# The transposes of an attention layer's keys and queries share the PSUM bank of the values' products

## The chip, the cores and the metric

The kernel runs on one core of a Trainium2 chip. The metric is the device time of one execution in microseconds; the kernel before took 1372.63 us in the median of three runs (1371.01 to 1373.25). The core has five engines that work side by side: TensorE (PE) multiplies matrices and writes only to PSUM, VectorE (DVE) and ScalarE (ACT) read PSUM and compute elementwise, GpSimd (POOL) does a little set-up, and SyncE (SP) issues the transfers. PSUM holds eight banks of 128 partitions by 512 float32 values in this kernel's tiles, and one tile takes one bank.

## What is computed

The reference is a decoder trunk of two layers over 512 tokens of width 1024. The first layer mixes two kinds of state-space heads, the second is a latent attention with 16 heads; each is followed by a SwiGLU network. The change is in the attention layer only:

```python
q = (rms_norm(cq, q_lora_norm) @ w_uq).reshape(bsz, seqlen, H, MLA_NOPE + MLA_ROPE)
kv = (rms_norm(ckv, kv_lora_norm) @ w_ukv).reshape(bsz, seqlen, H, MLA_NOPE + MLA_V)
...
s = jnp.einsum('bqhd,bkhd->bhqk', qn, k_nope) + jnp.einsum('bqhr,bkr->bhqk', qr, k_rope)
s = s.astype(jnp.float32) * scale
...
p = jax.nn.softmax(jnp.where(mask, s, -jnp.inf), axis=-1).astype(v.dtype)
return jnp.einsum('bhqk,bkhv->bqhv', p, v)
```

A head has 64 elements with a norm and 32 with a rotary position (the rotary key is shared by all heads), and its values have 64. The mask is causal.

## The kernel before

All tokens are one tile of 512 columns. A dense product in near float32 precision is done as three matmuls of the fp32r type: weight and activation are each split into a high and a low part, and high by high, high by low and low by high are added up in one accumulator (`mm3`, L149 to L152). The weights come by transfer into `wraw`, ACT rounds them to `whi` (L144) and DVE forms `wlo` (L145). The accumulators are a ring of three PSUM banks, `acc()` (L63), that the whole kernel uses.

The attention layer opens five more banks (L710): two for scores (`sco`), two for transposed probabilities (`ptr`) and one for the products of the values (`po`, reached by `aux("po")`). Three and five make eight: PSUM is full.

Heads are taken in pairs, eight pairs in all. `project(g)` (L826) makes queries, keys and values of two pairs with dense products, and then normalises them and applies the rotary part on DVE. `prepare` (L875) turns one pair's keys (one tile for both heads) and queries (one tile for each head) with PE transposes into three PSUM tiles. ACT and DVE copy the keys to `kT` (L886, L888), ACT copies the queries to `qT` (L894). There are four `kT` and four `qT` buffers, enough for two pairs. `attend` (L898) does four blocks of queries: scores (L911), mask and maximum on DVE (L914), exponential on ACT (L916), division on DVE (L922), transposes of the probabilities (L925) and a copy of them on ACT (L929). At the end come the products with the values in `po` (L934), and `split` empties that bank (ACT L126, then DVE L127). `o_round(r)` (L944) is the output projection over four pairs.

The code asks for the work in this order (L957 to L968): `project(0)`, `project(1)`, `prepare` of pair 0, and then for each pair p: `prepare` of pair p+1, `attend` of pair p, a `project` after pairs 0 and 2 (`PROJ`), and `o_round(0)` after pair 4. `o_round(1)` follows the loop.

Nothing in the code fixes the order within an engine. A planner takes, each time an engine is free in its own model of the times, the instruction that the code asked for first among those that are ready; the loading of weights is put 90 places ahead (`AHEAD`, L132). On the chip each engine then works through its list in that order, and waits on semaphores. A ring of PSUM banks is handed out in the order in which the code asks for its tiles: a tile waits until the one that had its bank has been read for the last time.

Of the kernel before, what the change touches and what calls it, by code (L numbers as in the profile page):

```python
# [46 lines left out]
def kernel(ctx: ExitStack, tc: tile.TileContext, A, yT, stop=99):  # L47
# [11 lines left out]
    def nm(s):  # L59
        cnt[0] += 1  # L60
        return f"{s}_{cnt[0]}"

    def acc():  # L63
        return pacc.tile([P, T], F32, tag="acc", name=nm("acc"))
# [11 lines left out]
    def aux(tag="st"):  # L76
        while isinstance(phase["tags"][tag], str):
            tag = phase["tags"][tag]
        return phase["p"].tile([P, T], F32, tag=tag, name=nm(tag), bufs=phase["tags"][tag])
# [17 lines left out]
    ps = acc()  # L97
# [3 lines left out]
    def col(name, i=0, lo=0, hi=P):  # L101
        j = PV[name] + i
        return pv[lo:hi, j:j + 1]
# [182 lines left out]
    with tc.tile_pool(name="gkp", bufs=1) as gkp:  # L286
        rtok = tok_scalar(R)

        ps = aux("a1")
# [15 lines left out]
        ps = aux()  # L305
# [26 lines left out]
        ps = aux()  # L332
# [6 lines left out]
        ps = aux()  # L339
# [168 lines left out]
        with tc.tile_pool(name="gla", bufs=2) as gp:  # L508
# [16 lines left out]
            for h in range(4):  # L525
                ps = aux()
# [186 lines left out]
    with tc.tile_pool(name="mla", bufs=2) as mp, tc.tile_pool(name="mla1", bufs=1) as m1:  # L713
# [30 lines left out]
        ps = acc()  # L744
# [10 lines left out]
        for who, n0, n in (("q", 0, 3), ("kv", 3, 2)):  # L755
            lora[who], ssq = [], None
            for c in range(n):
                w = weight(A["w_dqkv"][n0 + c], KD, P)
                ps = acc()
# [12 lines left out]
            ps = aux()  # L772
# [22 lines left out]
        ps = aux()  # L795
# [14 lines left out]
        ps = aux()  # L810
# [63 lines left out]

        def prepare(g, hp, qs, ks, v):  # L875

            ps = acc()
            for i in range(4):
                E.transpose(ps[:, i * P:(i + 1) * P],
                            ks[:, i, 2 * hp:2 * hp + 2, :].rearrange("p h d -> p (h d)"), ident)  # L880
            kts, qts = [], []
            for j in range(2):
                t = kT[(4 * g + 2 * hp + j) % NK]
                kts.append(t)
                if j == 0:
                    S.activation(t[0:64, :], ps[0:64, :], AF.Copy, scale=col("k_gain", 0, 0, 64))  # L886
                else:
                    V.tensor_scalar(t[0:64, :], ps[64:P, :], col("k_gain", 0, 64, P), None, ALU.mult)  # L888
            for j in range(2):
                ps = acc()  # L890
                for i in range(4):
                    E.transpose(ps[0:96, i * P:(i + 1) * P], qs[:, i, 2 * hp + j, :], ident)
                qT = mp.tile([96, T], F32, tag="qT", name=nm("qT"), bufs=4)
                S.activation(qT, ps[0:96, :], AF.Copy, scale=col("q_gain", 0, 0, 96))  # L894
                qts.append(qT)
            return kts, qts
# [59 lines left out]

        pr = {0: project(0), 1: project(1)}  # L957
        ready = prepare(0, 0, *pr[0])
        for p in range(8):
            g, hp = divmod(p, 2)  # L960
            cur = ready
            if p < 7:
                ready = prepare((p + 1) // 2, (p + 1) % 2, *pr[(p + 1) // 2])
            attend(g, hp, pr[g][2], *cur)
            if p in PROJ:
                pr[2 + PROJ.index(p)] = project(2 + PROJ.index(p))
            if p == 4:
                o_round(0)  # L968
# [89 lines left out]
```

## Time and profile before

| | |
|---|---|
| median of three runs | 1372.63 us |
| profiled execution, its own time | 1371.09 us |
| span from its first to its last instruction | 1368.9 us |
| PE busy | 1344.9 us, 98% |
| DVE, ACT busy | 815.5 us, 562.8 us |
| transposes of keys and queries | about 834 to 958 us of the span |
| products of the values (eight pairs) | 860.5 to 988 us |
| granted PE clock | 0.999 |

Times in the profile are counted from the span's first instruction. A row in order of time gives start, duration, engine, line, operation, the tiles written and read, shape and count; in brackets stands the idle time of the engine ahead of it and what ended that. Rows of one line that follow each other are merged. PEld is the loading of the stationary operand, which runs beside the matmuls. A matmul of float32 operands leaves two records.

### The profile page before, as it was taken

What the parts mean: (1) busy time and instruction counts of PE and PEld (TensorE: products, weight loads), DVE (VectorE), ACT (ScalarE), POOL (GpSimd) and SP (SyncE); (2) the same over time, 40 slices, a digit from 0 to 9 for tenths busy, and PEclk for the clock granted to TensorE, in tenths of its full rate; (3) what the DMA queues carried; (4) which work ended last, traced back from release to release, by engine and by line L of the source; (5) the groups of instructions that cost most, each with busy time, mean ns of one, the idle gap of its engine ahead of it and who ended that gap; (6) DMA issues with size and microseconds to landing.
All of it is one profiled execution on the core that took longest, in us unless ns stands there. A gap on an engine that the chain in (4) does not pass through costs nothing.

```text
span 1368.9 us, 16667 instructions
## 1 busy us (share of the span) xinstructions
PE 1344.9 (98%) x6506; PEld 1088.7 (80%) x6506; DVE 815.5 (60%) x1369; ACT 562.8 (41%) x941; POOL 7.8 (1%) x35
## 2 busy tenths in 40 slices
PE   8999999999999999999999999999999999999998
PEld 5788889788888888888888887666588888888887
DVE  7987976788867444444333469776594444443221
ACT  5584633544344322332232348775653322322121
POOL 0000000000000000000000000000000000000000
PEclk9999999999999999999999999999999999999999
DMA  5342232222233333223333321111033223323331
GB/s 177 109 141 91 77 95 78 78 77 62 79 93 105 93 94 106 92 92 99 90 100 100 101 68 56 39 47 62 1 98 103 93 93 102 98 93 108 111 103 63
DMA packets 36781, 122.22 MB, mean 89 GB/s; under 512 B 4768, under 2 KB 5792, under 8 KB 36704
## 3 DMA queue, kind: packets, MB, share of 16 engines
q1 hardware_dynamic: 35888, 120.72, 28.1%
q8 instruction: 51, 0.84, 0.2%
q10 hardware_dynamic: 816, 0.46, 0.1%
q14 instruction: 26, 0.21, 0.0%
HBM read 119.03 MB, written 2.13 MB: 89 GB/s over the span
## 4 chain that ended last, share of the span: by engine, by line
PE 90%; DVE 5%; ACT 3%; issue 1%; DMA 1%; SPq 0%; ACTq 0%
PE acc L150 27%; PE acc L151 27%; PE acc L152 27%; PE sco L911 2%; PE ptr L925 1%; PE po L934 1%; DVE wlo L145 1%; PE a L447 1%; PE a L625 0%; PE a L433 0%; PE a L614 0%; PE a L451 0%; ACT whi L144 0%; PE a L627 0%; DVE gm L534 0%
## 5 line engine op out<-in xcount | busy, mean ns | idle before, releaser
L150 PE MATMUL acc<-xh,whi 128*128 128x512 f32 x1144 | 449.1, 393 | 5.2 <-DVE dp L322 2.5
L144 ACT CAST whi<-wraw 128x1024 fp32r<-128x1024 f32 (+2 forms) x221 | 225.8, 1022 | 554.0 <-PE acc L151 436.9
L151 PE MATMUL acc<-xl,whi 128*128 128x512 f32 x1144 | 448.7, 392 | 0.0
L152 PE MATMUL acc<-xh,wlo 128*128 128x512 f32 x1144 | 448.7, 392 | 0.0
L145 DVE TENSOR_TENSOR wlo<-wraw,whi 128x1024 fp32r<-128x1024 f32 (+2 forms) x221 | 261.9, 1185 | 163.2 <-ACT whi L144 163.1
L150 PEld LDWEIGHTS acc<-xh,whi 128*128 128x128 f32 x1144 | 214.9, 188 | 51.2 <-ACT cvt L366 2.8
L152 PEld LDWEIGHTS acc<-xh,wlo 128*128 128x128 f32 x1144 | 215.1, 188 | 44.8 <-DVE wlo L145 0.6
L151 PEld LDWEIGHTS acc<-xl,whi 128*128 128x128 f32 x1144 | 215.1, 188 | 44.5 <-issue 1.4
L152 PE MATMUL acc<-fhh,wlo 128*128 128x512 f32 x288 | 112.0, 389 | 0.0
L150 PE MATMUL acc<-fhh,whi 128*128 128x512 f32 x288 | 112.0, 389 | 0.0
L151 PE MATMUL acc<-fhl,whi 128*128 128x512 f32 x288 | 112.0, 389 | 0.0
L683 DVE TENSOR_TENSOR fu<-acc,R 128x512 f32<-128x512 f32 x44 | 30.4, 691 | 136.2 <-PE acc L152 136.2
L680 DVE TENSOR_TENSOR fg<-acc,R 128x512 f32<-128x512 f32 x44 | 30.4, 691 | 89.0 <-PE acc L152 88.9
L152 PEld LDWEIGHTS acc<-fhh,wlo 128*128 128x128 f32 x288 | 54.1, 188 | 11.3
L151 PEld LDWEIGHTS acc<-fhl,whi 128*128 128x128 f32 x288 | 54.1, 188 | 11.3
L150 PEld LDWEIGHTS acc<-fhh,whi 128*128 128x128 f32 x288 | 54.1, 188 | 11.1
L151 PE MATMUL acc<-mxl,whi 128*128 128x512 f32 x128 | 49.9, 391 | 0.0
L150 PE MATMUL acc<-mxh,whi 128*128 128x512 f32 x128 | 49.8, 391 | 0.0
L152 PE MATMUL acc<-mxh,wlo 128*128 128x512 f32 x128 | 49.7, 390 | 0.0
L911 PE MATMUL sco<-kT,qT 96*128 96x128 f32 (+3 forms) x128 | 42.8, 445 | 1.5 <-DVE mx L914 1.3
L914 DVE CUSTOM_DVE_ANT_0 sc<-sco,am 128x128 f32<-128x128 f32 (+3 forms) x64 | 30.7, 487 | 13.6 <-PE sco L911 11.5
L916 ACT ACTIVATE sc<-sc,mx 128x128 f32<-128x128 f32 (+3 forms) x64 | 35.7, 561 | 7.3 <-DVE mx L914 6.8
(329 smaller groups left out, 1584.8 us busy)
## 6 DMA issues: line engine op xcount, KB each, us to landing
wraw<-in_w_gate_dram SPq DMA_DIRECT2D x44, 512.0 KB, 3.5
wraw<-in_w_up_dram SPq DMA_DIRECT2D x44, 512.0 KB, 3.5
wraw<-in_w_down_dram SPq DMA_DIRECT2D x32, 512.0 KB, 3.6
wraw<-in_w_out_dram SPq DMA_DIRECT2D x16, 512.0 KB, 3.6
wraw<-in_w_xbc_dram SPq DMA_DIRECT2D x12, 512.0 KB, 3.6
wraw<-in_w_down_dram SPq DMA_DIRECT2D x16, 384.0 KB, 3.1
wraw<-in_w_z_dram SPq DMA_DIRECT2D x8, 512.0 KB, 3.5
wraw<-in_w_v_dram SPq DMA_DIRECT2D x8, 512.0 KB, 3.5
```

The costliest lines, as they stand in the source:

```text
L144: S.copy(hi[:, :kc * m], r)
L145: V.tensor_tensor(lo[:, :kc * m], r, hi.bitcast(F32)[:, :kc * m], ALU.subtract)
L150: E.matmul(out, ah, bh, start=first, stop=False)
L151: E.matmul(out, ah, bl, start=False, stop=False)
L152: E.matmul(out, al, bh, start=False, stop=last)
L447: E.matmul(pd[64 * h:64 * h + 64, c * P:(c + 1) * P], xdt[:, c, h, :], mt[:, h, c, :], start=True, stop=True)
L680: V.tensor_tensor(g, pg, R, ALU.mult)
L683: V.tensor_tensor(u, pu, R, ALU.mult)
L911: E.matmul(ps[:, :n], qts[j][:, b * P:(b + 1) * P], kts[j][:, :n], start=True, stop=True)
L914: V.tensor_tensor_reduce(sc[:, :n], ps[:, :n], am[:, T - n:], -scale, 3e38, ALU.add, ALU.min, mx[:, j:j + 1])
L916: S.activation(sc[:, :n], sc[:, :n], AF.Exp, bias=mx[:, j:j + 1], scale=-1.0, accum_out=sm[:, j:j + 1])
L925: E.transpose(ps[:, kb * P:(kb + 1) * P], sc[:, kb * P:(kb + 1) * P], ident)
```

## The change

The three PSUM tiles of `prepare` (one of keys, two of queries) are taken from the bank `po` instead of from the three accumulators. `po` has one bank. Everything else is as it was.

```diff
         def prepare(g, hp, qs, ks, v):
 
-            ps = acc()
+            ps = aux("po")
             for i in range(4):
                 E.transpose(ps[:, i * P:(i + 1) * P],
                             ks[:, i, 2 * hp:2 * hp + 2, :].rearrange("p h d -> p (h d)"), ident)
...
             for j in range(2):
-                ps = acc()
+                ps = aux("po")
                 for i in range(4):
                     E.transpose(ps[0:96, i * P:(i + 1) * P], qs[:, i, 2 * hp + j, :], ident)
                 qT = mp.tile([96, T], F32, tag="qT", name=nm("qT"), bufs=4)
```

## The prediction

> **What bounds the kernel now.** I read the page first (shares, the chain of work that ended last), then the busy time by stretches of the attention stage, then what TensorE (PE) waited for there, then single rows in order of time.
>
> ```profile
> span 1368.9 us, 16667 instructions
> ...
> PE 1344.9 (98%) x6506; PEld 1088.7 (80%) x6506; DVE 815.5 (60%) x1369; ACT 562.8 (41%) x941; POOL 7.8 (1%) x35
> ...
> PE 90%; DVE 5%; ACT 3%; issue 1%; DMA 1%; SPq 0%; ACTq 0%
> ```
>
> PE is busy 98% of the span and is 90% of the chain. The change adds and removes no instruction, so it can move the time only through PE's idle time, 1368.9 - 1344.9 = 24.0 us in all, and only where keys and queries are transposed. Busy time by stretch (length, then PE, PEld, DVE, ACT, POOL, granted clock):
>
> ```profile
> 834.00:842.00 8.00, 5.71 (x38) 4.35 (x36) 7.81 (x19) 6.73 (x12) 0.00 (x0) 1.00 0.36 115
> 842.00:864.00 22.00, 21.55 (x116) 16.35 (x117) 18.35 (x51) 19.54 (x45) 0.00 (x0) 1.00 0.19 58
> 864.00:878.00 14.00, 11.36 (x55) 7.39 (x53) 13.10 (x46) 8.33 (x24) 0.00 (x0) 1.00 0.10 39
> 878.00:900.00 22.00, 21.90 (x123) 15.07 (x122) 14.79 (x42) 18.34 (x45) 0.00 (x0) 1.00 0.15 49
> 900.00:914.00 14.00, 10.97 (x54) 6.68 (x53) 10.77 (x38) 11.37 (x30) 0.00 (x0) 1.00 0.12 38
> 914.00:948.00 34.00, 34.00 (x173) 24.69 (x173) 22.25 (x54) 14.83 (x36) 0.00 (x0) 1.00 0.13 44
> 948.00:962.00 14.00, 12.88 (x73) 9.07 (x72) 10.62 (x36) 11.49 (x32) 0.00 (x0) 1.00 0.16 47
> 962.00:989.00 27.00, 26.23 (x142) 15.44 (x140) 14.56 (x54) 17.52 (x51) 0.00 (x0) 1.00 0.01 1
> sum 155.00, PE 144.60 PEld 99.05 DVE 112.25 ACT 108.14 POOL 0.00; mean PE 18.07 PEld 12.38 DVE 14.03 ACT 13.52 POOL 0.00
> ```
>
> PE idles 155.00 - 144.60 = 10.4 us here: 2.3 at the start, 2.6 in 864 to 878, 3.0 in 900 to 914, 1.1 in 948 to 962, next to nothing elsewhere. What PE waited for in 834 to 992 (total, times, longest):
>
> ```profile
> PE acc L150 <- ACT qT L894: 3.0, 2, 1.6
> PE acc L879 <- ACT qT L894: 1.4, 3, 1.0
> PE acc L150 <- ACT qs L838: 0.7, 1, 0.7
> PE acc L892 <- DVE kT L888: 0.6, 1, 0.6
> PE acc L892 <- ACT v L852: 0.6, 1, 0.6
> PE acc L150 <- DVE kT L888: 0.5, 1, 0.5
> ```
>
> These six are waits for an accumulator bank to be emptied, 3.0 + 1.4 + 0.7 + 0.6 + 0.6 + 0.5 = 6.8 us, two thirds of the idle time. Why a bank is late is seen at the second pair of 860 to 878. Here prepare(n) is the preparation of pair n and po(n) its product of values; below, a hop is the hand-over of a bank from one tile to the next:
>
> ```profile
> 860.50 2.37 PE L934 MATMUL po<-pt,v 128*64 128x512 f32 x16
> ...
> 864.88 0.66 PE L879 MATMUL acc<-ident,ks 128*128 128x128 f32 x4 [0.21 <-ACT qT L894]
> ...
> 873.17 0.45 PE L150 MATMUL acc<-whi,lh 128*128 128x384 f32 x1 [1.35 <-ACT qT L894]
> ...
> 875.69 0.44 PE L150 MATMUL acc<-whi,lh 128*128 128x384 f32 x1 [0.67 <-ACT qs L838]
> ...
> 882.52 2.37 PE L934 MATMUL po<-pt,v 128*64 128x512 f32 x16
> ...
> 893.55 2.38 PE L934 MATMUL po<-pt,v 128*64 128x512 f32 x16
> ```
> ```profile
> 863.09 0.60 ACT L126 CAST xh<-po 128x512 fp32r<-128x512 f32 x1
> ...
> 871.87 0.68 ACT L886 ACTIVATE kT<-acc,pv 64x512 f32<-64x512 f32 x1 [0.17 <-PE sco L911]
> 872.45 0.67 ACT L894 ACTIVATE qT<-acc,pv 96x512 f32<-96x512 f32 x1
> ...
> 877.21 0.68 ACT L894 ACTIVATE qT<-acc,pv 96x512 f32<-96x512 f32 x1 [0.98 <-PE sco L911]
> ```
>
> prepare(3) fills three accumulators from 864.88 on, but its kT and qT buffers still belong to pair 1, whose scores come first (the releaser is the score matmul, L911). So the banks are emptied only from 871.87 to 877.89, and project(3), whose dense products stand behind them, can't start before 873.17. Three of three accumulators are parked for 7 to 13 us.
>
> **The change, part by part.** Removed: 8 x 3 = 24 claims on the accumulators. Added: 24 claims on the one bank of po, which had 8, so 32 claims in one line. Instructions, shapes, DMAs and their queues stay. The bank is handed out in the order in which the code asks: prepare(n+1) sits between po(n-1) and po(n). Nothing is parked any more: when po(n-1) is done, the scores of pair n-1, which held kT and qT, are done too.
>
> *Start* (834 to 842). Six tiles go out here, with these waits:
>
> ```profile
> 835.09 0.60 PE L879 MATMUL acc<-ident,ks 128*128 128x128 f32 x4
> 836.24 1.05 PE L892 MATMUL acc<-ident,qs 128*96 128x128 f32 x8 [0.55 <-ACT v L852]
> 838.27 0.66 PE L879 MATMUL acc<-ident,ks 128*128 128x128 f32 x4 [0.98 <-ACT qT L894]
> 840.15 0.64 PE L892 MATMUL acc<-ident,qs 128*96 128x128 f32 x4 [0.56 <-DVE kT L888]
> ```
> ```profile
> 836.68 0.95 DVE L145 TENSOR_TENSOR wlo<-wraw,whi 128x768 fp32r<-128x768 f32 x1
> ...
> 839.34 0.75 DVE L888 TENSOR_SCALAR kT<-acc,pv 64x512 f32<-64x512 f32 x1
> ...
> 859.51 0.56 DVE L145 TENSOR_TENSOR wlo<-wraw,whi 128x384 fp32r<-128x384 f32 x1 [0.81 <-ACT whi L144]
> ...
> 864.57 0.68 DVE L127 TENSOR_TENSOR xl<-po,xh 128x512 fp32r<-128x512 f32 x1
> ...
> 949.94 1.23 DVE L145 TENSOR_TENSOR wlo<-wraw,whi 128x1024 fp32r<-128x1024 f32 x1 [0.16 <-ACT whi L144]
> ```
>
> Before: 0.55 + 0.98 + 0.56 = 2.1 us idle. After: the first queries wait for the keys' second copy on DVE, which is behind other work there until 839.34 and ends at 840.1. Meanwhile project(2) may have the accumulators, but its first split weight is ready only at 836.68 + 0.95 = 837.6, while the keys' transposes end at 835.7: some 1.7 to 1.9 us idle. Gain 0.3; bounds 2.1 (all goes) and -1.0 (the delayed first scores hold up pair 0).
>
> *864 to 878.* The waits 0.21 + 1.35 + 0.67 = 2.2 us. project(3) can fill them: its queries' weights are split by 859.51 + 0.56 = 860.1, and the next stretch (21.90 of 22.00) shows that what is pulled forward shortens a full one. Gain 2.2; bounds 0 and 2.2.
>
> *900 to 914.* The one wait of 1.60:
>
> ```profile
> 913.82 0.50 PE L150 MATMUL acc<-xh,whi 128*128 128x512 f32 x1 [1.60 <-ACT qT L894]
> ...
> 951.12 0.66 PE L879 MATMUL acc<-ident,ks 128*128 128x128 f32 x4 [0.20 <-ACT qT L894]
> ...
> 959.42 0.47 PE L150 MATMUL acc<-xh,whi 128*128 128x512 f32 x1 [0.47 <-DVE kT L888]
> ```
>
> o_round(0) then has three accumulators at once and 3 banks x 3 ready inputs x 3 matmuls = 27 dense matmuls to put into its gaps. But pair 3 is itself bound by its chain through DVE and ACT here, and dense work used early is missing at 914 to 921. Gain 1.1; bounds 0 and 3.0 (all idle time of this stretch).
>
> *Tail* (948 to 989). 0.20 + 0.47 = 0.7 us; I take 0.5. The lower bound is -2: prepare(7) moves from 951 to behind po(5), towards pair 7's first scores.
>
> *The new waits.* A hop puts the next tile on PE behind one copy on ACT (0.68) or DVE (0.76), and behind the waiting transpose stands all that PE has queued. Its cover is dense work ordered in between; without cover the hop costs the copy, some 0.8 us. From the trace: the six tiles of the start, with no cover, waited 2.1 us (0.35 each); the other 18 waited 0.21 + 0.20 (0.02 each). 24 claims of the 32 lie outside the start (18 tiles and 6 products that take turns): 0.5 us by the one, 8.4 by the other. They are nearer to the covered ones, as o_round and project now always have banks; I take 0.04, so 1.0 us.
>
> A row first, then a rule: after the start, PE's waits ahead of the transposes themselves are two, each 0.2 us. The Trainium skill ("Perfetto Trace Analysis", Optimization Strategy) says that the same gap repeating on the engine that should be saturated can mean too little PSUM for the next tile, buffer count included. By that rule the present gaps would point to the accumulators, and one bank for 32 claims would make a new row of gaps; the second reading is the slower rival below. The trace can't yet decide it.
>
> *Is there time for the line of hops?* Emptying po: from 862.87 to the end of xl at 865.25, 2.4 us. Then keys 0.6 + 0.76 + 0.1 and twice queries 0.6 + 0.68 + 0.1: 4.2 us. Together 6.6 us between two products. The shortest gap that has a preparation in it is 884.89 to 893.55, 8.7 us. So po isn't late, with 2 us to spare.
>
> **Sum.** 0.3 + 2.2 + 1.1 + 0.5 - 1.0 = 3.1 us. The profiled execution took 1371.09 us (2.19 around the span) and would take 1368.0; it lies 1.54 under the median shown, 1372.63, so a median run would take **1369.5 us**.
>
> **The rivals.**
> *Gaps only move.* Dense work is finite: what is pulled into 864 to 878 and 900 to 914 is missing later, where the chain of a pair (scores, DVE, ACT, transposes, products) sets the pace. For it: ACT or DVE is above 80% busy in most stretches. Against: 878 to 900 and 914 to 948 are full of PE work. Only the 864 stretch pays, less the hops and half of it given back: 2.2 / 2 - 0.5 = 0.6 us faster, 1372.0. That the planner orders all so that the change does next to nothing is in this case too.
> *All goes.* The 6.8 us go but for the 1.7 of the start, the rest of the idle time of 900 to 914 (3.0 - 1.6 = 1.4) is filled, and the hops cost the lower price: 6.8 - 1.7 + 1.4 - 0.5 = 6.0 us faster, 1366.6. For it: three free accumulators wherever dense work is left. Against: it has to be left just there.
> *Slower: the hops are uncovered.* prepare(n+1) in the one bank holds up po(n): four hops in a row after each product, each a copy behind ACT's or DVE's own queue, and PE in order behind it. The price by the start's 0.35 is 8.4; gains of 4.1 against it: 4.3 us slower, 1376.9. It decides from 4.1 / 24 = 0.17 us a hop; the 2 us to spare are used up when each of the four is 0.5 us late. For it: one split of a weight keeps DVE for 1.23 us (949.94), and L888 can stand behind it. Against: the rows of 0.02. At 0.29 a hop the price is 7.0 and the time 1375.5.
>
> **How the numbers follow.** Forecast 0.42 (its own range 1368.3 to 1371.0), gaps only move 0.23, all goes 0.17, slower 0.18. A measurement of this kernel tells some 0.2% (2.7 us) from no change, so faster means under 1369.9: all goes 0.17 and a little over half of the forecast, 0.25, make 0.42; the rest of it and gaps only move make 0.40; slower 0.18. The range of 8 in 10 reaches into both ends: 1366.0 to 1375.5.
>
> **What would show it.** Right: PE's waits for qT (L894) ahead of L150 at about 873 and 914 are gone, project(3)'s first dense matmul starts near 862 to 866, transposes of a pair follow each product by 2 to 3 us, and PE's idle time from 834 to 989 falls from 10.4 to about 7. Wrong: PE waits in rows like po <- qT, po <- kT or po <- xl of more than 4 us in all, or PE idle near 10 us with gaps at new places.

## The result, and the profile after

The change made the kernel slower: 1382.26 us in the median (1381.34 to 1382.64) against 1372.94 us of the kernel before on the same chip (1371.01 to 1373.93). The ratio is 1.0069, with a 95% interval of 1.0054 to 1.0084. The forecast was 1369.5 us, in a range of 1366.0 to 1375.5.

The page of the changed kernel, its span and two of its lines:

```profile
span 1379.9 us, 16666 instructions
...
PE 1351.5 (98%) x6506; PEld 1093.5 (79%) x6506; DVE 816.9 (59%) x1369; ACT 562.0 (41%) x941; POOL 7.8 (1%) x35
...
PE 90%; DVE 5%; ACT 2%; DMA 1%; issue 1%; SPq 0%; ACTq 0%
```

These lines hardly differ from those of before: PE is 98% busy in both. Its busy time itself has grown, from 1344.9 to 1351.5 us, with the same 6506 matmuls. The rows are longer, so the question is also one of PE's clock.

To compare like with like I call *the stage* the stretch from the first transposes of keys to the last matmul that waits for the split of the last product (the L150 row behind ACT's `xh`). It holds everything that the change touches. Here it is as one row each, of the kernel before and of the changed kernel (stretch, length, then busy time and records of PE, PEld, DVE, ACT and POOL, granted clock, share of DMA, GB/s):

```profile
835.09:989.14 154.05, 143.51 (x756) 98.23 (x754) 111.17 (x334) 107.50 (x267) 0.00 (x0) 1.00 0.13 42
```
```profile
837.28:1000.24 162.96, 147.28 (x757) 100.67 (x755) 112.38 (x334) 106.82 (x267) 0.00 (x0) 0.96 0.12 40
```

The stage is 162.96 - 154.05 = 8.9 us longer. PE's idle time went from 154.05 - 143.51 = 10.5 to 162.96 - 147.28 = 15.7 us, which is 5.1 of it, and its busy rows grew by 147.28 - 143.51 = 3.8 us with the granted clock down from 1.00 to 0.96. The rest of the two spans' difference, 11.0 us, is a start that lies 2.2 us later, ahead of the first changed instruction. Most of that arose between 40 and 60 us, where the granted clock was 0.91 in this execution and 1.00 in that of the kernel before (82 matmuls got done there against 90); traces of other kernels below have the same dip there (keys alone) or lack it (queries alone), so I don't count it to the change.

The stage of the changed kernel in parts, in the same columns:

```profile
837.28:846.60 9.32, 8.13 (x50) 6.77 (x48) 8.84 (x25) 5.87 (x9) 0.00 (x0) 1.00 0.30 100
846.60:850.40 3.80, 0.03 (x1) 0.00 (x0) 3.74 (x6) 1.03 (x3) 0.00 (x0) 0.84 0.00 0
850.40:858.00 7.60, 7.57 (x24) 4.75 (x25) 5.01 (x18) 5.28 (x16) 0.00 (x0) 0.63 0.09 26
858.00:880.00 22.00, 22.00 (x119) 15.85 (x118) 16.38 (x52) 19.04 (x47) 0.00 (x0) 1.00 0.22 73
880.00:885.20 5.20, 2.30 (x14) 1.78 (x12) 5.20 (x12) 1.22 (x4) 0.00 (x0) 1.00 0.00 0
885.20:892.00 6.80, 6.35 (x28) 4.35 (x30) 4.30 (x19) 4.10 (x12) 0.00 (x0) 0.75 0.00 0
892.00:928.00 36.00, 32.57 (x174) 22.91 (x170) 26.59 (x78) 27.57 (x67) 0.00 (x0) 1.00 0.14 45
...
992.00:1000.24 8.24, 5.61 (x28) 2.56 (x26) 1.07 (x4) 2.49 (x6) 0.00 (x0) 0.79 0.00 0
```

Three places stand out: 3.8 us without a matmul at 846.6, a half-empty stretch at 880, and the end from 992. Behind the first two, and within the third, the clock is below 1 (0.63, 0.75, 0.79), while DMA is next to nothing: no transfer is in the way. What PE waited for (total, times, longest):

```profile
PE ptr L925 <- DVE sc L922: 6.2, 3, 2.9
PE po L892 <- DVE kT L888: 4.0, 2, 3.8
...
PE po L892 <- ACT qT L894: 0.4, 1, 0.4
```

The waits for an accumulator that I had listed (`acc` behind `qT`, `qs` and `kT`) are gone, as forecast. In their place stand one wait of 3.8 us for the copy of the keys and three waits for DVE's division of the probabilities.

The rows around the two long waits, PE first (start, duration, engine, line, operation, tiles, shape; in brackets the idle time ahead and what ended it):

```profile
845.37 0.60 PE L879 MATMUL po<-ident,ks 128*128 128x128 f32 x4
845.80 0.82 PE L911 MATMUL sco<-kT,qT 96*128 96x128 f32 x4
850.43 0.45 PE L892 MATMUL po<-ident,qs 128*96 128x128 f32 x1 [3.81 <-DVE kT L888]
...
881.96 0.34 PE L152 MATMUL acc<-whi,ll 128*128 128x384 f32 x1
885.24 0.52 PE L925 MATMUL ptr<-ident,sc 128*128 128x128 f32 x3 [2.94 <-DVE sc L922]
```

DVE and ACT in the same stretch, and ACT where `project(3)`'s first accumulators are emptied:

```profile
845.36 1.22 DVE L865 TENSOR_TENSOR qs<-qs,hry 128x1024 f32<-128x1024 f32 x1
846.50 0.68 DVE L868 TENSOR_TENSOR rr<-qs,hry 128x512 f32<-128x512 f32 x1
847.10 1.22 DVE L872 TENSOR_TENSOR ks<-ks,hry 128x1024 f32<-128x1024 f32 x1
...
849.62 0.76 DVE L888 TENSOR_SCALAR kT<-po,pv 64x512 f32<-64x512 f32 x1
...
880.53 1.23 DVE L865 TENSOR_TENSOR qs<-qs,hry 128x1024 f32<-128x1024 f32 x1
...
884.68 0.41 DVE L922 TENSOR_SCALAR sc<-sc,sm 128x384 f32<-128x384 f32 x1
```
```profile
846.97 0.67 ACT L886 ACTIVATE kT<-po,pv 64x512 f32<-64x512 f32 x1
851.56 0.68 ACT L894 ACTIVATE qT<-po,pv 96x512 f32<-96x512 f32 x1 [3.93 <-PE po L892]
853.60 0.68 ACT L894 ACTIVATE qT<-po,pv 96x512 f32<-96x512 f32 x1 [0.48 <-PE po L892]
854.18 0.56 ACT L838 ACTIVATE qs<-acc,lry 128x384 f32<-128x384 f32 x1
...
899.88 0.67 ACT L894 ACTIVATE qT<-po,pv 96x512 f32<-96x512 f32 x1
900.45 1.04 ACT L838 ACTIVATE qs<-acc,lry 128x384 f32<-128x384 f32 x2
```

Two things are to be read here. First, the one bank: the keys of pair 1 are in it at 846, ACT copies its half by 847.6, but DVE's half (L888) stands in DVE's list behind the normalisation of `project(1)` (from L865 at 845.36 on) and begins only at 849.62. The queries want the same bank and wait. The wait of 2.94 us has the same block ahead of it: the division (L922, 884.68) stands behind the normalisation of `project(2)` (from 880.53 on). So does the third in length, 2.08 us at 928.15, behind that of `project(3)` (from 922.65 to the division at 927.53).

Second, `qs`. It has two buffers, and `project(n+2)` fills the one of `project(n)`. L838, which empties an accumulator into it, may start only when the last transpose (L892) has read the old content. In this trace L838 follows the last `qT` of pair 1 (853.60, then 854.18) and again the last `qT` of pair 3 (899.88, then 900.45). Until then three finished accumulators stay full, and there is no dense matmul that PE could do while a bank is late: the last one before the first wait ends at 845.5, with the next at 856.11, and the last one before the second ends at 882.3, with the next at 901.72, behind L838 at 900.45. In the kernel before, the queries of pair 3 went through the accumulators ahead of that, and L838 came at 875.

### The profile page after: what moved, and what is told of

Same layout as the page of the kernel before. It is cut to its first block, busy times and chain, and to the rows that moved or that the text cites. A ratio compares the mean times of both kernels' runs of the same rounds, so it can differ in the third digit from the quotient of the medians.

```text
span 1379.9 us, 16666 instructions
## 1 busy us (share of the span) xinstructions
PE 1351.5 (98%) x6506; PEld 1093.5 (79%) x6506; DVE 816.9 (59%) x1369; ACT 562.0 (41%) x941; POOL 7.8 (1%) x35
## 4 chain that ended last, share of the span: by engine, by line
PE 90%; DVE 5%; ACT 2%; DMA 1%; issue 1%; SPq 0%; ACTq 0%
PE acc L150 27%; PE acc L151 27%; PE acc L152 26%; PE sco L911 2%; PE po L934 1%; PE ptr L925 1%; PE a L447 1%; DVE wlo L145 1%; PE po L892 1%; PE a L625 0%; PE a L433 0%; PE a L614 0%; DMA x<-in_xT_dram 0%; PE a L451 0%; ACT pt L929 0%
## 5 line engine op out<-in xcount | busy, mean ns | idle before, releaser
L150 PE MATMUL acc<-xh,whi 128*128 128x512 f32 x1144 | 450.4, 394 | 3.2 <-DVE dp L322 2.5
L150 PEld LDWEIGHTS acc<-xh,whi 128*128 128x128 f32 x1144 | 215.3, 188 | 49.6 <-ACT cvt L366 2.9
L150 PE MATMUL acc<-fhh,whi 128*128 128x512 f32 x288 | 112.0, 389 | 0.0
L150 PEld LDWEIGHTS acc<-fhh,whi 128*128 128x128 f32 x288 | 54.1, 188 | 11.3
L150 PE MATMUL acc<-mxh,whi 128*128 128x512 f32 x128 | 49.7, 391 | 0.0
L911 PE MATMUL sco<-kT,qT 96*128 96x128 f32 (+3 forms) x128 | 46.4, 466 | 0.8 <-ACT qT L894 0.8
L914 DVE CUSTOM_DVE_ANT_0 sc<-sco,am 128x128 f32<-128x128 f32 (+3 forms) x64 | 30.9, 488 | 13.9 <-PE sco L911 8.6
```

The costliest lines, as they stand in the source:

```text
L150: E.matmul(out, ah, bh, start=first, stop=False)
L911: E.matmul(ps[:, :n], qts[j][:, b * P:(b + 1) * P], kts[j][:, :n], start=True, stop=True)
L914: V.tensor_tensor_reduce(sc[:, :n], ps[:, :n], am[:, T - n:], -scale, 3e38, ALU.add, ALU.min, mx[:, j:j + 1])
```

## The experiments

Theory A says that the second reading is the cause: the one bank delays the transposes of the queries, so `qs` isn't free, so the accumulators stay full, so PE has nothing to put between the hops. Theory B says that the hop itself is the price: a transpose stands in PE's list behind a copy that stands in DVE's list. The expectations of the first four runs (each half alone, the two banks, the copy on ACT) name theories of their own, in which `qs` had no part yet. Each time is a median, and each ratio is against the kernel before on the same chip (it isn't always quite the quotient of the two medians). Idle times and rows are of the one profiled execution of each kernel.

### One part of the change alone

Only the keys through `po` (against the kernel before):

```diff
-            ps = acc()
+            ps = aux("po")
             for i in range(4):
                 E.transpose(ps[:, i * P:(i + 1) * P],
                             ks[:, i, 2 * hp:2 * hp + 2, :].rearrange("p h d -> p (h d)"), ident)
```

> Keys through the bank of po, queries from the accumulators again. Theory of the line: the 3.81 us stall after the change is the first queries of pair 1 waiting behind the keys' second copy, which stands on DVE behind the normalisation of project(1). With the queries in other banks they don't wait for it, so that stall and the lowered clock behind it go: 1372 to 1376 us. Rival, the new order of the dense products is what costs, whatever bank the transposes use: some 1379 to 1383 us, with gaps at the same places.

Measured: 1365.02 us, ratio 0.9941 (0.9922 to 0.9959). The stage takes 145.26 us with 4.4 us idle. So half of the change is a gain. Neither theory foresaw it: the time lies 7 us below the lower of the two ranges. It has the hops of the keys and DVE's copy in them, and no wait above 0.7 us. L838 of `project(3)` comes at 875.04 here.

Only the queries through `po` (against the kernel before):

```diff
             for j in range(2):
-                ps = acc()
+                ps = aux("po")
                 for i in range(4):
                     E.transpose(ps[0:96, i * P:(i + 1) * P], qs[:, i, 2 * hp + j, :], ident)
```

> Queries through the bank of po, keys from the accumulators again. Theory of the line: the bank is emptied by ACT alone, which isn't behind the normalisation, so each hop costs about 0.7 us and no stall of 3 us arises; 1371 to 1376 us. Should the line itself cost, with any tile in it, then over 1378 us. Rival, the order: 1379 to 1383 us.

Measured: 1370.45 us, ratio 0.9976 (0.9965 to 0.9987). The stage takes 153.08 us with 7.7 us idle, and has a drop of the clock. L838 of `project(3)` comes only at 893.81 here, and the longest wait is 2.34 us. Neither half alone loses.

### Two banks instead of one

```diff
-            ps = aux("po")
+            ps = aux("ptr")
```

(for all three tiles; `ptr` has two banks)

> All three tiles of a pair through the two banks of the transposed probabilities instead of the one of po. Theory of the line: with two banks and no product of values in the ring a tile waits for the copy before the last only; keys can still be held up by DVE, but one of the two banks goes on: 1371 to 1377 us. Rival, accumulators free of transposes make the planner run project(n) ahead and put normalisation before the pairs' own work, whatever bank is used: 1379 to 1383 us, gaps before L925 as after the change.

Measured: 1374.37 us, ratio 1.0009 (0.9996 to 1.0022); stage 155.90 us, 10.5 us idle. A second bank takes the loss away, but doesn't give the gain that the keys alone give. L838 of `project(3)` comes at 889.77.

### The copy off DVE

```diff
-                    V.tensor_scalar(t[0:64, :], ps[64:P, :], col("k_gain", 0, 64, P), None, ALU.mult)
+                    S.activation(t[0:64, :], ps[64:P, :], AF.Copy, scale=col("k_gain", 0, 64, P))
```

> The kernel after, but the second head's keys are copied by ACT instead of DVE; the line of 32 claims stays. Theory of the line behind DVE: the stall of 3.81 us goes and about 3 us of lowered clock with it, so 1374 to 1378 us; the later gaps, where the probabilities' division stands behind the normalisation, may stay. If the line itself costs: no better than 1380 us. Rival, the order: 1380 to 1383 us.

Measured: 1373.2 us, ratio 1.0006 (0.9996 to 1.0015). The wait of 3.81 us is gone and the loss with it; the time lies 0.8 us below the range of 1374 to 1378 us. Taken alone this speaks for theory B. The same edit on the kernel before is its control:

> The kernel before with the keys' second copy on ACT instead of DVE: control of the same edit on the changed kernel (1373.2). If the loss of the changed kernel is that this copy stands in DVE's list behind the normalisation, the edit gains nothing here, 1371 to 1376 us. If ACT is simply the better engine for it, it gains as much here, 1363 to 1367.

Measured: 1366.95 us, ratio 0.9959 (0.9943 to 0.9975). The edit makes the kernel before 0.41% faster too, and the changed kernel 1.0006 / 1.0069 = 0.9937, 0.63% faster (plus or minus 0.18%; for ratios of ratios I take the root of the sum of the squared half widths). The part that belongs to the one bank alone is 0.2%, no more than the uncertainty (0.24%). So the time of this run doesn't show that the loss is the copy behind the normalisation: the edit is worth about as much where no such wait is. Whether ACT is the better place for the copy, or each of the two new plans is a lucky one, isn't shown.

### The order in the bank turned round

```diff
+            kts, qts = [], []
+            for j in range(2):
+                ps = aux("po")
+                for i in range(4):
+                    E.transpose(ps[0:96, i * P:(i + 1) * P], qs[:, i, 2 * hp + j, :], ident)
...
             ps = aux("po")
             for i in range(4):
```

Both query tiles go first, and the keys' tile after them.

> The changed kernel with the order in the bank turned round: both query tiles first, then the keys' tile, all through po. Theory A: the queries leave qs before the slow keys' copy on DVE, the accumulators are emptied earlier, 1370 to 1376 us, idle time of the stage 9 to 12 us. Theory B: the number of hops and the copies are the same, and the product then waits for the keys' copy on DVE instead of the queries waiting for it: 1378 to 1384 us, idle time 14 to 16 us.

Measured: 1373.02 us, ratio 0.9988 (0.9977 to 0.9998); stage 152.64 us, 10.0 us idle. The number of hops and of copies is the same and the loss is gone, in the range of theory A. But the rows bear that theory out only in part: `project(2)`'s accumulators are emptied from 848.28 on, against 854.18, while those of `project(3)` still wait until 891.54 and then go three in one go, against 900.45. What is gone is the wait behind the slow copy, since the queries no longer stand behind it. That the plan is another one as well is a caution which the next runs bear out.

### A third buffer for qs

A third buffer needs 6 KB more in each partition, which had to be freed: the rotary scratch goes into the tile of squares, and the rotary key into the buffer of `kT3`. That makes the planner order the work anew, so there is a control with the same space and two buffers.

```diff
-        krr = m1.tile([32, T], F32, name="krr")
+        krr = m1.tile([96, T], F32, tag="kT3", name="krr")[0:32, :]
...
-            rr = mp.tile([P, 16, 32], F32, tag="rr", name=nm("rr"), bufs=1)
+            s2 = sq.rearrange("p a b -> p (a b)")
+            rr = s2[:, 0:512].rearrange("p (a b) -> p a b", a=16)
+            rt = s2[:, 512:1024].rearrange("p (i h d) -> p i h d", i=4, h=4)
...
-            qs = mp.tile([P, 4, 4, 96], F32, tag="qs", name=nm("qs"))
+            qs = mp.tile([P, 4, 4, 96], F32, tag="qs", name=nm("qs"), bufs=3)
```

The control has all of it but the last line.

> The changed kernel with scratch space shared (the rotary scratch lies in the tile of squares, the rotary key in a kT tile), queries' buffer qs still two deep: a control for the next run. Both theories: as the changed kernel, 1380 to 1384 us, PE idle 15 to 16 us in its 163 us from the first transposes to the last product's split, granted clock at about 0.6 for some 7 us after the first long wait.

> The changed kernel with a third buffer for the queries qs (space as in the control). Theory A (the one bank delays the query transposes, so qs is not free, L838 of the next projection can't empty its three accumulators, and PE has no dense work to put between the hops): PE's wait of 3.8 us for the keys' copy at 850 shrinks below 1 us, dense matmuls run between 846 and 854 and between 882 and 901, idle time of the stage 15.7 -> 8 to 11 us, no drop of the granted clock; 1370 to 1375 us. Theory B (the hop itself: a transpose stands in PE's list behind a copy that stands in DVE's list behind the normalisation; accumulators don't matter): the waits of 3.8, 2.9 and 2.1 us stay, idle time 14 to 16 us, 1378 to 1383 us.

The control took 1374.45 us, ratio 0.9998 (0.9989 to 1.0008), and with the third buffer the changed kernel took 1364.89 us, ratio 0.9929 (0.9915 to 0.9944). The stage of the control, and that of the kernel with the third buffer, in one row each:

```profile
837.77:993.07 155.30, 144.61 (x757) 100.45 (x755) 110.86 (x334) 107.96 (x268) 0.00 (x0) 0.98 0.13 42
```
```profile
835.44:982.08 146.64, 140.86 (x757) 97.39 (x755) 110.05 (x334) 107.87 (x268) 0.00 (x0) 1.00 0.14 44
```

ACT's rows in the control, where L838 of the edited file is L839 and L894 is L897, and then in the kernel with the third buffer:

```profile
851.48 0.68 ACT L897 ACTIVATE qT<-po,pv 96x512 f32<-96x512 f32 x1 [0.58 <-PE po L895]
852.07 1.50 ACT L839 ACTIVATE qs<-acc,lry 128x384 f32<-128x384 f32 x3
```
```profile
838.96 0.57 ACT L839 ACTIVATE qs<-acc,lry 128x384 f32<-128x384 f32 x1
...
841.89 1.04 ACT L839 ACTIVATE qs<-acc,lry 128x384 f32<-128x384 f32 x2
```

With two buffers three accumulators are emptied in one go behind the last `qT`, at 852; with three they are emptied at 839 and 842, as they fill. Idle time falls from 10.7 to 5.8 us, the clock stays at 1.00, and PE's waits for the bank in the whole stage shrink to one:

```profile
PE po L895 <- DVE kT L891: 0.7, 1, 0.7
```

That is the mechanism of theory A, with a larger gain than it had: the time lies 5 us below its range, the idle time 2 us below. It isn't the hop that became cheaper. In the control, too, PE waits only 0.9 us for the copies of the keys; what goes with the third buffer is 1.6 us of waits for L839, 2.5 of the 4.4 us of waits for DVE's maximum and division, and the low clock (0.98 to 1.00). What I had not expected is the control: it differs from the changed kernel in the place of scratch alone and is 0.9998 / 1.0069 = 0.9929 of its time. In its plan the copy of the keys comes at 848.58, ahead of the normalisation, and the wait of 3.8 us isn't there. So a plan can make or take away as much as the whole loss, and the next runs ask how far that goes.

### The same space and depth on the kernel before

> The kernel before with the same sharing of scratch space, qs two deep: the control of the next run. The order of the work is planned anew, so a few us either way: 1368 to 1377 us.

> The kernel before (all three tiles through the accumulators) with a third qs buffer. Theory A1 (a third qs frees accumulators only where the query transposes come late, which is a thing of the one bank): no change against its control, within 3 us of it, PE idle in the stage 9 to 11 us. Theory A2 (qs two deep held back the projections of the kernel before as well): 5 to 9 us below its control, 1363 to 1368 us, and then the change of banks has nothing of its own to do with the gain.

Measured: 1380.15 us for the control, ratio 1.0048 (1.0031 to 1.0065), and 1379.31 us with a third buffer, ratio 1.0044 (1.0029 to 1.0058). The third buffer gives the kernel before nothing, 0.9996 (plus or minus 0.0022): theory A1. But both are slower than the kernel before itself, by a plan of their own, and the control lies 3 us above the range that I had given it; their idle time (13.8 and 13.9 us) lies above the 9 to 11 us of A1. Rows of PE and of DVE in the kernel before with three buffers (L866 and L917 are L865 and L914 of the unedited file):

```profile
871.00 0.66 PE L928 MATMUL ptr<-ident,sc 128*128 128x128 f32 x4 [0.25 <-ACT pt L932]
875.75 2.07 PE L914 MATMUL sco<-kT,qT 96*128 96x512 f32 x2 [4.10 <-DVE mx L917]
```
```profile
870.99 1.22 DVE L866 TENSOR_TENSOR qs<-qs,hry 128x1024 f32<-128x1024 f32 x1
...
875.14 0.55 DVE L917 CUSTOM_DVE_ANT_0 sc<-sco,am 128x384 f32<-128x384 f32 x1
```

The score matmul waits 4.10 us for a bank that DVE (L917) is to read, and in DVE's list stands the normalisation again (from 870.99 on), this time ahead of the scores. It is the same accident as the 3.81 us of the changed kernel, at another place and with the accumulators' banks.

### The copy off DVE with three buffers

> The kernel before with a third qs buffer and the keys' second copy on ACT. If the 4.1 us wait of a score matmul for DVE and the half clock behind it were all that made the third-buffer version of the kernel before slow, and the new plan is without it: about 1371 to 1373 (1379.3 less 4.1 less 3.4). If the accumulators alone are enough once qs is free: 1364 to 1367.

> The changed kernel with a third qs buffer and the keys' second copy on ACT. With qs free there is dense work for PE while a copy is late, so where the copy runs is worth little: 1362 to 1367 us, PE idle in the stage 4 to 7 us, no drop of the clock. Were the hop itself the price, the edit would gain again some 3 us: 1361.

Measured: 1371.91 us for the kernel before so edited, ratio 0.9996 (0.9985 to 1.0007), and 1366.04 us for the changed kernel, ratio 0.9944 (0.9924 to 0.9964). Neither has a wait above 1.6 us in the stage. So here the change of banks is compared without the accident on either side.

### What the change of banks is worth in five plans

Each row is the same edit, accumulators to `po`, made on another surrounding:

| surrounding | accumulators | `po` | `po` to accumulators | PE idle in the stage, us |
|---|---|---|---|---|
| as it was | 1.0000 | 1.0069 | 1.0069 ± 0.0015 | 10.5 and 15.7 |
| key copy on ACT | 0.9959 | 1.0006 | 1.0047 ± 0.0019 | 7.6 and 9.0 |
| shared space, two `qs` | 1.0048 | 0.9998 | 0.9950 ± 0.0019 | 13.8 and 10.7 |
| three `qs` | 1.0044 | 0.9929 | 0.9886 ± 0.0021 | 13.9 and 5.8 |
| three `qs`, key copy on ACT | 0.9996 | 0.9944 | 0.9948 ± 0.0023 | 9.4 and 6.7 |

With two `qs` buffers the sign depends on the plan. With three it is a gain in both plans, 0.5% without the accident. The third buffer itself is worth 0.9929 / 0.9998 = 0.9931 (plus or minus 0.0017) with `po` and nothing with the accumulators.

### Two banks, and only the keys, with three buffers

> All three tiles through the two banks of the transposed probabilities, with a third qs buffer. If the one bank's line of hops still costs something once qs is free, two banks are 1 to 3 us below the one bank with a third buffer (1364.9): 1361 to 1364. If the line costs nothing more: 1364 to 1366.

> Only the keys go through po, the queries through the accumulators, and qs has a third buffer. Theory A: the queries leave qs early already when they go through the accumulators, so a third buffer gives nothing more: 1363.5 to 1367 us, stage idle 4 to 6 us. Theory B: the same, 1365 us.

> Keys through po, queries through the accumulators, third qs buffer, the keys' second copy on ACT. As the same without the last edit (1364.0), within 2 us: 1362 to 1366.

Measured: 1365.77 us (0.9941, 0.9925 to 0.9958) for the two banks of `ptr`; 1364.02 us (0.9921, 0.9903 to 0.9939) for the keys alone through `po`; 1365.39 us (0.9942, 0.9923 to 0.9961) for that with the copy on ACT. Stages of 146.62, 146.75 and 145.96 us, idle 5.0, 5.2 and 5.7 us. Once `qs` is free, one bank is as good as two, and it matters little which tiles go where: with the two versions above, five lie between 0.9921 and 0.9944. The keys alone, with two `qs` buffers and a one-line edit (1365.02, 0.9941), already beat both kernels by as much; these versions can't be told apart.

Plans differ, so the twelve kernels with some or all of these tiles off the accumulators are best read as two groups, by the time at which the first accumulator of `project(3)` is emptied into `qs` (L838, or L839 where `qs` has been edited, in us of each trace):

| kernel | first emptied at | ratio |
|---|---|---|
| three `qs`: all to `po`; the same, key copy on ACT; all to `ptr` | 866.32; 874.86; 871.20 | 0.9929; 0.9944; 0.9941 |
| three `qs`: keys to `po`; the same, key copy on ACT | 868.98; 872.82 | 0.9921; 0.9942 |
| two `qs`: keys to `po` | 875.04 | 0.9941 |
| two `qs`: all to `ptr`; queries first; queries to `po` | 889.77; 891.54; 893.81 | 1.0009; 0.9988; 0.9976 |
| two `qs`: key copy on ACT; shared space | 895.24; 898.23 | 1.0006; 0.9998 |
| two `qs`: the changed kernel | 900.45 | 1.0069 |

The groups don't overlap, 0.9921 to 0.9944 against 0.9976 to 1.0069, over twelve plans. The keys alone, with two `qs` buffers, belong to the faster group, as theory A has it, since their queries still leave early. So late queries with two `qs` buffers cost the gain that the change could have had. Within the second group only the changed kernel is slower than the kernel before by more than its interval, and it alone has a wait of more than 2.6 us.

### Pauses put into TensorE

To measure the clock by itself, six pauses were put into the first feed-forward stage of the kernel before:

```diff
+        for _ in range(n):
+            j = V.tensor_scalar(pause, pause, 1.0, None, ALU.mult)
...
+        m = E.matmul(ps[:, 0:P], ident, pause[:, 0:P], start=True, stop=True)
```

The chain has 2, 3, 4, 5, 6 or 8 operations; the small matmul `m` waits for it, and the next dense matmul for `m`.

> The kernel before with six pauses of TensorE put into the first feed-forward stage, each a chain of 2, 3, 4, 5, 6 or 8 DVE operations that the next dense matmul waits for (estimate 0.4 to 0.8 us an operation by DVE's rows of 128 by 512: pauses of 1 to 6 us). Clock theory C1 (the clock falls only behind a pause of more than 3.4 us, as behind the 3.81 us at 847): no drop behind the shorter pauses, half clock for some 3.5 us behind the longer. Clock theory C2 (it falls behind any pause of 2 us or more): a drop behind nearly all six. A drop costs about half its length, 1.5 to 2 us, on top of the pause.

Measured: 1414.84 us in one execution, 40.9 above the kernel before. Each pause and the stretch behind it, of three of the six:

```profile
460.91:464.15 3.24, 0.00 (x2) 0.03 (x1) 3.10 (x5) 1.31 (x2) 0.00 (x0) 1.00 0.09 6
464.15:467.70 3.55, 3.55 (x10) 2.90 (x11) 0.76 (x2) 0.21 (x1) 0.00 (x0) 0.52 0.40 142
498.90:502.65 3.75, 0.00 (x1) 0.03 (x1) 3.67 (x7) 1.52 (x2) 0.00 (x0) 0.88 0.09 32
502.65:508.40 5.75, 5.75 (x15) 4.59 (x16) 0.61 (x2) 0.00 (x0) 0.00 (x0) 0.50 0.18 72
...
658.80:665.33 6.53, 0.00 (x1) 0.03 (x1) 6.17 (x12) 1.52 (x2) 0.00 (x0) 0.76 0.23 82
665.33:669.00 3.67, 3.67 (x10) 2.99 (x11) 0.16 (x1) 0.00 (x0) 0.00 (x0) 0.50 0.00 0
```

All six pauses (3.24, 3.75, 4.68, 5.14, 5.60 and 6.53 us) came out longer than estimated, and all are followed by half clock, for 2.9 to 5.8 us of full work. The pauses add up to 28.9 us, and the loaded stretches lose 12.2 us (length times one minus the clock, over all six): 41.1 together, for the 40.9 measured. (The kernel before varies from 1370.88 to 1375.62 us on that chip, so one execution can't vouch for so close an agreement.) A pause thus costs its length and some 2 us more. The shortest, 3.24 us, already lies under the 3.4 of C1; a shorter one is in the last section.

## Why the prediction was wrong

The step that failed is the cover of the hops: "o_round and project now always have banks", and with it the price of 0.04 us a hop. Two buffers of `qs` kept `project`'s finished accumulators full until the late queries had been read, so there was no dense work to cover a hop, and one hop alone waited 3.8 us, where the sum had 1.0 us for all 24. Idle time was to fall by 3.1 us and rose by 5.1; the clock, for which there was no term, took about 3.8 us more. Term by term:

**What bounds the kernel** held: nothing but PE's idle time in the stage and, which I had not counted, its clock there.

**Start: gain 0.3.** Right up to the second pair. In 837.28 to 846.60 PE idles 9.32 - 8.13 = 1.2 us against 2.3 before, a gain of 1.1, and 1.05 us of what is left is the wait for `project(2)`'s first split weight, as forecast. Then the keys of pair 1 cost 3.8 us, far past the lower bound of -1.0.

**864 to 878: gain 2.2.** The same failure, in the sentence "project(3) can fill them: its queries' weights are split". The waits did go (858 to 880 has 22.00 of 22.00), but 880 to 892 idles 12.00 - 2.30 - 6.35 = 3.4 us, more than the 2.7 us between 864 and 900 before. I took a free accumulator and split weights as all that a projection needs. It needs a place to be emptied to as well. I had read the code's statement that the tiles of `prepare(3)` now sit behind `po(1)`, and counted it as "nothing is parked any more"; what it moved is the last read of `project(1)`'s `qs`, from 868.0 (L892, before) to 899.6, so the accumulators were parked again, this time by finished sums of `project(3)`.

**900 to 914: gain 1.1.** Not seen: 892 to 928 idles 36.00 - 32.57 = 3.4 us, against 3.1 between 878 and 948 before.

**Tail: gain 0.5, lower bound -2.** Idle time is 2.6 us in the last 8.24 us, against 0.8 us in the last 8.14 us before (981.00 to 989.14), and the clock is 0.79 against 1.00, worth another 0.21 x 8.24 = 1.7 us; together they went past the lower bound. The last dense matmul ahead of the end starts at 992.10 here, while before there were some up to 985.66 to fill the stretch: this much is the first rival, dense work used early and missing later.

**New waits: 1.0 us, at 0.04 a hop.** The waits ahead of the transposes in `po` are 4.0 + 0.4 = 4.4 us, and 3.8 of them are one hop. With three `qs` buffers, where the cover holds, the same hops wait 0.7 us; but with two of them and the shared space, where the accumulators are full as well, they wait no more than 1.9 us (0.9, 0.6 and 0.4). So the want of dense work alone doesn't make the long wait: the copy has to be late in DVE's list too. The other end of my bound, 8.4 us as 24 times 0.35, was no better picture: the price doesn't come in equal parts, it is one stand of DVE's normalisation.

**Is there time for the line of hops.** Yes, as computed: `po` was never late for its products. I asked what the line makes late for `po` and didn't ask what it makes late for the other buffers that its tiles read.

**Clock.** There was no term for it. It is about 3.8 of the stage's 8.9 us.

**The rivals.** "The hops are uncovered" named the right side, the right engine and the place ("L888 can stand behind it"), with a chance of 0.18 and 1376.9 us: 5 us too little. It had the split of a weight, 1.23 us, as the worst that could stand ahead of the copy; 4.3 us of normalisation stood there (845.36 to 849.62). It had no term for the clock either. Of the signs that I wrote down as wrong, both came: more than 4 us of waits for the bank (4.4), and gaps at new places, with PE idle for even more than the 10 us that I named (15.7).

The rule of the Trainium skill that I quoted ("Perfetto Trace Analysis", Optimization Strategy) names SBUF beside PSUM when it says that a repeating gap can mean too few buffers. I weighed it for PSUM alone. The runs agree with the half that I left out: a third buffer of `qs`, which lies in SBUF, took 9.6 us off its control (1374.45 to 1364.89), and a second PSUM bank on top of it took off nothing (1365.77).

**What is settled and what isn't.** Shown: the tie of the accumulators to the query transposes, by the rows of L838 and by the two groups of twelve kernels; the plans with late queries and two `qs` buffers, other than the changed kernel, lie 0.3 to 0.9% above the others. Shown too: a wait of some 4 us with low clock behind it is in the changed kernel's plan and not in that of the kernel before, and other plans have it the other way round. Not settled is how much of the measured 0.69% that one wait and the clock behind it make: every edit that takes it away takes the loss away, but the copy on ACT helps the kernel before as well, and each such edit makes a new plan, worth up to 0.7% by itself.

## What to carry to other kernels

When a ring of PSUM banks is relieved by moving some tiles to another bank, follow each moved tile to the buffer that it reads, and ask who is waiting to write there: an accumulator isn't free until it can be emptied. Price a hand-over with the largest block that can stand ahead of the copy in its engine's list, once, and not with a mean over many. Where a planner orders the work, try the same edit in several surroundings before believing a difference of less than 1%: here one edit gave between +0.7% and -1.1%.

## What the runs showed of the hardware

PE's granted clock halves after a stretch of little work and stays there for several microseconds of full work. Taking the low clock as 0.5, the rows of the pauses say when: in the one of 6.53 us the clock was low for 0.24 x 6.53 / 0.5 = 3.1 us, so it fell 3.4 us after the last matmul, and with the 3.67 us behind it was low for 6.8 us. Over the six pauses it fell 2.6 to 4.1 us after the last matmul and was low for 3.4 us (two of them) or 6.7 to 6.8 us (four). Matmuls of 128x512 that start every 0.23 us at full clock start every 0.43 us there; two rows ahead of the first pause, and two behind the second:

```profile
460.07 0.39 PE L159 MATMUL acc<-xh,whi 128*128 128x512 f32 x1
460.30 0.39 PE L162 MATMUL acc<-xl,whi 128*128 128x512 f32 x1
...
504.07 0.63 PE L163 MATMUL acc<-xh,wlo 128*128 128x512 f32 x1
504.50 0.63 PE L159 MATMUL acc<-xh,whi 128*128 128x512 f32 x1
```

It doesn't take an empty stretch. With only the queries through `po`, the longest wait in this place is 2.34 us, and PE is busy for 0.84 of 3.80 us:

```profile
873.20:877.00 3.80, 0.84 (x6) 0.41 (x5) 3.80 (x11) 0.51 (x2) 0.00 (x0) 1.00 0.00 0
877.00:885.00 8.00, 8.00 (x29) 6.26 (x29) 4.94 (x19) 5.09 (x16) 0.00 (x0) 0.57 0.00 0
```

The 8.00 us behind it ran at 0.57. The kernel before kept the full clock through a stretch with more work, 2.46 of 4.00 us:

```profile
837.00:841.00 4.00, 2.46 (x20) 1.96 (x19) 3.87 (x10) 3.31 (x7) 0.00 (x0) 1.00 0.58 177
841.00:850.00 9.00, 8.54 (x45) 7.19 (x44) 8.56 (x28) 6.58 (x16) 0.00 (x0) 1.00 0.07 25
```

The longest wait doesn't decide it. The wait of 1.60 us that ends at 913.82 in the kernel before left the clock at 1.00, while in the kernel before with three buffers and the copy on ACT waits of at most 1.60 us were followed by half clock:

```profile
838.00:842.60 4.60, 1.29 (x8) 0.81 (x8) 2.71 (x5) 4.54 (x8) 0.00 (x0) 0.97 0.50 185
842.60:845.60 3.00, 2.96 (x13) 2.83 (x14) 1.62 (x8) 2.96 (x5) 0.00 (x0) 0.50 0.00 0
```

So theory C1 of the pauses is too strict: what went with the clock is PE's work in some 4 us. But in the two stretches that lost the clock this work was transposes alone (L925 in the first, L882 and L895 in the second), and in the one that kept it there were score matmuls (L911) as well, so amount and kind of work aren't told apart here. The Trainium skill ("TensorE: Matmul & The Clock Gate", Part 1: The HAM clock gate) gives a window of about 3.4 us, half rate after an idle one and full rate after a busy one; the lengths of the slow stretches, 3.4 and 6.8 us, agree with one and two such windows, but a window without any work is more than it took here: 22% busy, with transposes, was enough.
